# Up projections of the second layers' MLPs as seven products of quarter matrices, with weight sums made by DMA in DRAM

## The chip, the cores and the metric

One core of one Trainium2 chip runs the whole program. The metric is the device time of one execution in microseconds (us). The engines are PE (TensorE; PEld is its weight load), DVE (VectorE), ACT (ScalarE), POOL (GpSimd) and SP (SyncE, which only issues DMAs here). P is 128, S is 512 tokens, D is 1024.

## The reference

A block of a first type (pooling, stick-breaking attention, gates, an MLP) is followed by two layers of a second type. What the change touches is the MLP at the end of each second-type layer:

```python
D_FF_2 = 2816
    for l in range(DEPTH_2):                      # 2 layers
        ...
        h2 = _rmsnorm(x, g_ffn[l])
        z = _dwconv(h2 @ w_up[l], w_dw_ffn[l], b_dw_ffn[l])   # 1024 -> 5632, 3 taps along the tokens
        zg, zv = jnp.split(z, 2, axis=-1)
        x = x + (jax.nn.silu(zg) * zv) @ w_down[l]            # 2816 -> 1024
    return _rmsnorm(x, g_final)
```

All inputs and outputs are float32. The 5632 columns of `w_up` are 22 pairs of 128 gate columns and 128 value columns.

## The kernel before

Activations lie as [channels, tokens], so 1024 channels are eight tiles of 128x512. Every float32 product is made of three products of rounded parts: an operand is split into a high part `hi` (a cast to fp32r) and a low part `lo` (the remainder), and `mm3` (lines 376 to 380) issues hi·hi (L378), hi·lo (L379) and lo·hi (L380) into the same PSUM bank.

Weights come in units of eight blocks of 128x128, in the order in which PE uses them. `weight_plan` writes that order down as a list of units; the host packs the array `w` by it. `prep` brings one unit in: SP loads 512 KB into one of three `raw` buffers (L356), ACT casts it to `whi` (L357), POOL subtracts to get `wlo` (L358); `whi` and `wlo` have four buffers each. `take` hands out the next block and calls `prep` for units up to three ahead (`AHEAD`). There are 301 units. A unit's 24 products of 512 columns are PE's work between two units.

A scheduler orders each engine's queue: an instruction may be placed ahead of others that stand before it in the program, if it needs nothing from them. PE alone follows the program's order where `tc.manual_schedule` says so. Each queue then runs strictly in that order, and an instruction that waits for a semaphore holds what is behind it. DMAs that SP and ACT issue share eight completion semaphores in turn.

The program begins with `block1`: about 213 us of attention over eight heads, in which PE alternates between the heads (`scores`, `sums`, `weigh`, `mix_values`) and projections that fill its waits. ACT works there for each head through the three banks zC, zB, zA (L641, L342, L647), and this is what PE's next step waits for. Units 0 to 27 belong to this stretch. Its MLP and two calls of `layer2` follow.

At the end of `layer2` stands the MLP of the change. The first two column pairs are made by `proj_outer` (four banks at once, eight k steps), then `fin` gives the norm factor `r`; the other pairs are two `proj` of eight blocks each. Per pair, two multiplications by `r` (L1279), the three-tap filter `conv3` (L1282 to L1284) on both halves, a Silu, a product (L1298) and a split into `ah`, `al` (L446, L447) follow on ACT and DVE. After 11 pairs come the down projections into eight tiles of `x`, then the other 11 pairs.

## Time and profile before

| | |
|---|---|
| median of 3 runs | 1894.17 us (1893.68 to 1894.34) |
| profiled execution, its own time | 1894.09 us |
| its span, first to last instruction | 1892.4 us |
| mean granted TensorE clock | 0.994 |
| busy: PE, PEld, DVE, ACT, POOL | 97%, 79%, 51%, 50%, 50% |
| HBM read, written | 161.37 MB, 2.10 MB |

The page gives the busy time of each engine, then the span in 40 slices (a digit is the busy share in tenths), the DMA queues, the chain of work that ended last, and the costliest groups of instructions. Other views of the trace give one stretch: its instructions in order of time, its busy times, or who waited for whom. A matmul's printed duration overlaps the next one's, so PE's pace is read from the distance between starts.

### The profile page before, as it was taken

The page shows a single profiled execution, that of the slowest core. Times are in us where ns is not written, and L with a number is a line of the kernel's source. Part 1 is how long each engine was busy: PE and PEld are TensorE (multiplying, and loading weights), DVE is VectorE, ACT ScalarE, POOL GpSimd, SP SyncE. Part 2 cuts the span into 40 slices and gives each one's busy share as a digit, 9 for nine tenths or more (in the row PEclk, how much of TensorE's full clock was granted, in tenths as well). Part 3 has the DMA queues.
Part 4 walks back from the last instruction along what each step waited for, and adds up shares of the span by engine and source line. Part 5 has one row for each costly group of instructions (what it writes and reads, how often), then busy time and mean ns, then how long its engine had stood idle before and what let it go on. Part 6 is the DMA issues. An engine that isn't in the chain of part 4 may idle for free. (4 is left out here: it accounts for less than half of the span.)

```text
span 1892.4 us, 22115 instructions
## 1 busy us (share of the span) xinstructions
PE 1844.0 (97%) x8448; PEld 1500.1 (79%) x8448; DVE 959.7 (51%) x1420; ACT 948.1 (50%) x1442; POOL 937.1 (50%) x510
## 2 busy tenths in 40 slices
PE   8999999999999999899999999999999999999997
PEld 6877888888888888666788888888866788888886
DVE  4666552724032038996565225522998365405543
ACT  6766633633233347597554224434778554324442
POOL 5233444644444558665544444455866464444442
PEclk9999999999999999999999999999999999999999
DMA  5111224222222222200232222222210122222221
GB/s 186 68 56 61 79 101 140 89 101 91 99 100 90 100 79 90 78 27 23 87 110 93 97 101 97 92 100 93 97 39 23 61 101 100 92 98 100 95 96 56
DMA packets 48649, 164.89 MB, mean 87 GB/s; under 512 B 5536, under 2 KB 7584, under 8 KB 48544
## 3 DMA queue, kind: packets, MB, share of 16 engines
q1 hardware_dynamic: 46304, 160.34, 24.5%
q10 hardware_dynamic: 2240, 3.15, 0.5%
q8 instruction: 66, 1.08, 0.2%
q14 instruction: 39, 0.32, 0.1%
HBM read 161.37 MB, written 2.10 MB: 86 GB/s over the span
## 5 line engine op out<-in xcount | busy, mean ns | idle before, releaser
L358 POOL TENSOR_TENSOR wlo<-raw,whi 128x1024 fp32r<-128x1024 f32 x300 | 720.7, 2404 | 817.5 <-ACT whi L357 813.6
L357 ACT CAST whi<-raw 128x1024 fp32r<-128x1024 f32 (+1 forms) x302 | 313.7, 1040 | 507.5 <-PE b L379 412.7
L378 PE MATMUL b<-xh,whi 128*128 128x512 f32 (+1 forms) x1296 | 495.3, 382 | 2.7 <-ACT xh L449 2.7
L379 PE MATMUL b<-xl,whi 128*128 128x512 f32 (+1 forms) x1296 | 491.7, 379 | 3.4 <-DVE xl L450 3.3
L380 PE MATMUL b<-xh,wlo 128*128 128x512 f32 (+1 forms) x1296 | 491.3, 379 | 0.0
L379 PEld LDWEIGHTS b<-xl,whi 128*128 128x128 f32 x1296 | 244.3, 189 | 51.6 <-DVE xl L450 4.4
L378 PEld LDWEIGHTS b<-xh,whi 128*128 128x128 f32 x1296 | 244.2, 188 | 50.4 <-ACT xh L449 3.1
L380 PEld LDWEIGHTS b<-xh,wlo 128*128 128x128 f32 x1296 | 244.3, 189 | 45.9
L378 PE MATMUL b<-ah,whi 128*128 128x512 f32 (+1 forms) x646 | 243.6, 377 | 0.0
L379 PE MATMUL b<-al,whi 128*128 128x512 f32 (+1 forms) x646 | 243.2, 377 | 0.0
L380 PE MATMUL b<-ah,wlo 128*128 128x512 f32 (+1 forms) x646 | 243.2, 376 | 0.0
L380 PEld LDWEIGHTS b<-ah,wlo 128*128 128x128 f32 x646 | 121.6, 188 | 22.4
L378 PEld LDWEIGHTS b<-ah,whi 128*128 128x128 f32 x646 | 121.6, 188 | 22.3
L379 PEld LDWEIGHTS b<-al,whi 128*128 128x128 f32 x646 | 121.6, 188 | 22.2
L1218 POOL TENSOR_TENSOR cacc<-cacc,pd 128x510 f32<-128x510 f32 (+14 forms) x94 | 120.4, 1281 | 32.0 <-ACT pd L1216 28.3
L1206 DVE SCALAR_TENSOR_TENSOR cv<-u,vec,cv 128x497 f32<-128x497 f32 (+13 forms) x146 | 108.3, 742 | 7.7 <-ACT cv L1196 5.5
L1279 DVE TENSOR_TENSOR b<-b,r 128x512 f32<-128x512 f32 x88 | 61.0, 697 | 97.1 <-PE b L380 96.9
L1303 DVE TENSOR_TENSOR x<-x,b 128x512 f32<-128x512 f32 x30 | 20.6, 687 | 161.3 <-PE b L380 161.3
L446 ACT CAST ah<-cg 128x512 fp32r<-128x512 f32 x44 | 27.3, 621 | 98.7 <-DVE cg L1298 98.7
L378 PE MATMUL mm<-xh,whi 128*128 128x512 f32 x176 | 69.4, 394 | 0.0
L869 DVE TENSOR_TENSOR b<-rl,b 128x512 f32<-128x512 f32 x32 | 22.1, 695 | 92.6 <-ACT rl L868 92.6
L379 PE MATMUL mm<-xl,whi 128*128 128x512 f32 x176 | 68.8, 391 | 0.0
(430 smaller groups left out, 2851.1 us busy)
## 6 DMA issues: line engine op xcount, KB each, us to landing
raw<-w SPq DMA_DIRECT2D x295, 512.0 KB, 3.2
x<-xT SPq DMA_DIRECT2D x8, 256.0 KB, 6.6
x<-xT ACTq DMA_DIRECT2D x8, 256.0 KB, 4.8
raw<-w SPq DMA_DIRECT2D x7, 256.0 KB, 2.6
outT<-o ACTq DMA_DIRECT2D x4, 256.0 KB, 2.4
outT<-o SPq DMA_DIRECT2D x4, 256.0 KB, 2.5
vec<-vec SPq DMA_DIRECT2D x1, 363.0 KB, 6.9
f<-pos SPq DMA_DIRECT2D x1, 256.0 KB, 3.3
```

Source lines behind the costliest of these rows:

```text
L357: nc.scalar.copy(out=hi[:, cs], in_=raw[:, cs])
L358: (eng or nc.gpsimd).tensor_tensor(out=lo[:, cs], in0=raw[:, cs], in1=hi[:, cs].bitcast(F32), op=ALU.subtract)
L378: mm(ps, lhsT=wb[0], rhs=xb[0], start=start, stop=False, **kw)
L379: mm(ps, lhsT=wb[0], rhs=xb[1], start=False, stop=False, **kw)
L380: mm(ps, lhsT=wb[1], rhs=xb[0], start=False, stop=stop, **kw)
L446: nc.scalar.copy(out=hi, in_=src)
L869: V.tensor_tensor(out=ps, in0=rl, in1=ps, op=ALU.mult)
L1206: V.scalar_tensor_tensor(out=acc[:, o], in0=us[i][:, u], scalar=self.v("w_dw_conv_2", l, i * CONV_K + k), in1=acc[:, o], op0=ALU.mult, op1 ...
L1218: G.tensor_tensor(out=acc[:, o], in0=acc[:, o], in1=pd, op=ALU.add)
L1279: V.tensor_tensor(out=ps, in0=ps, in1=r, op=ALU.mult)
L1303: V.tensor_tensor(out=self.x[m], in0=self.x[m], in1=ps, op=ALU.add)
```

## The change

Nineteen of the 22 pairs of each layer (all but the first three, `PLAIN2`) are computed as a 2x2 block product in seven quarter products in place of eight. The weight of a pair is cut into four quarters of 512x128 (a11, a12 gate and value columns of the upper half of the 1024 channels; a21, a22 of the lower half), the normed activations into four quarters of 512x256 (halves of channels and of tokens). A quarter product is four blocks with 256 columns each, three matmuls per block.

- **Weights.** A new input `wq` holds the quarters. Four sums per pair are needed (S1 = a21 + a22, S3 = a11 + a21, S2 = S1 + a11, S4 = S2 + a12; the signs are put elsewhere). They are made in DRAM, for groups of four pairs (1.05 MB; the last group has three, 0.79 MB): a copy DRAM to DRAM issued from ACT, then a DMA issued from POOL that adds the second term to what the copy wrote. That is 20 copies and 20 adds for each layer, 40 and 40 in all. The program calls them one by one from `prep`, from unit 24 on, every second unit for layer 0 and every third for layer 1.
- **Units.** A pair takes 28 blocks in place of 16, so there are 359 units in place of 301. A unit with quarters is loaded by two or three DMAs of 2 KB rows.
- **Activations.** `quarter_inputs` makes the seven right-hand operands (four normed quarters and their differences, each split into parts), on DVE, ACT and POOL, while PE runs `proj_outer` for the three plain pairs (six banks). The matmul that sums the squares now stands after two of the eight k steps.
- **Pairs.** A pair's products accumulate in two banks, and intermediate sums are read out while the bank goes on being filled: three half-bank copies on ACT (`snap`), three half-bank adds on DVE. The multiplications by `r` are gone for these pairs. PE runs the last two products of a pair between those of the next one.
- **Chunks** are 8, 7 and 7 pairs in place of 11 and 11, so three rounds of down projections; the first three tiles of a round are interleaved. The order on PE is now written by hand for the whole MLP.

```diff
-CHUNK2 = 11
+CHUNKS2 = (0, 8, 15, 22)
+PLAIN2 = 3
+NDOWN = 3
+SUM_PAIRS = 4
+SUMS = ("S1", "S2", "S3", "S4")
+QUARTERS = ("a11", "a12", "a21", "a22")
+SIDE_FROM, SIDE_STEPS = 24, (2, 3)
...
+        ffn = [("w_up_2", l, P * k, _span(P * f + o)) for k in range(KT) for f in range(PLAIN2) for o in (0, FF2)]
+        for ks in chunks2():
+            quarter = lambda which, f: [(which, l, f, kk) for kk in range(KT // 2)]
+            before = None
+            for f in ks:
+                if f >= PLAIN2:
+                    ffn += quarter("a11", f) + quarter("a12", f)
+                    if before is not None:
+                        ffn += quarter("a22", before)
+                    ffn += quarter("S2", f) + quarter("S1", f)
+                    if before is not None:
+                        ffn += quarter("S4", before)
+                    ffn += quarter("S3", f)
+                    before = f
+            down = [("w_down_2", l, P * k, _span(P * m)) for k in ks for m in range(NDOWN)]
+            ffn += down[:4] + quarter("a22", before) + down[4:8] + quarter("S4", before) + down[8:]
+            ffn += [("w_down_2", l, P * k, _span(P * m)) for m in range(NDOWN, KT) for k in ks]
+        add(ffn)
...
+def pack_quarters(inputs):
+    w = inputs["w_up_2"].reshape(NL, 2, KT // 2, P, 2, NF2, P)[:, :, :, :, :, PLAIN2:]
+    w = w.transpose(0, 4, 1, 5, 3, 2, 6)
+    return np.ascontiguousarray(w).reshape(NL, 4, NF2 - PLAIN2, P, KT // 2 * P)
...
+        if eng is None and any(b[0] in QUARTERS + SUMS for b in self.plan[u]):
+            for c0, c1, src in self.sources(u):
+                nc.sync.dma_start(out=raw[:, c0:c1], in_=src)
...
+        if u >= SIDE_FROM and self.side and u % SIDE_STEPS[self.side[0][0]] == 0:
+            self.side.popleft()[1]()
...
+    def sources(self, u):
+        out = []
+        for b, (name, l, f, kk) in enumerate(self.plan[u]):
+            if name in QUARTERS:
+                src = self.wq[l, QUARTERS.index(name), f - PLAIN2]
+            elif name in SUMS:
+                reg, i = divmod(f - PLAIN2, SUM_PAIRS)
+                src = self.sum_of[l, name, reg].rearrange("r (x c) -> (r x) c", c=KT // 2 * P)[i * P : (i + 1) * P]
...
+        nc = self.nc
+        pool = ctx.enter_context(self.tc.tile_pool(name="sums", bufs=1, space=bass.MemoryType.DRAM))
+        self.sum_of = {}
+        row = 2048
+        n = NF2 - PLAIN2
+        for l in range(NL):
+            regs = [(i, min(i + SUM_PAIRS, n)) for i in range(0, n, SUM_PAIRS)]
+            quarter = lambda name, r: self.wq[l, QUARTERS.index(name), r[0] : r[1]].rearrange("a p c -> (a p c)").rearrange("(r c) -> r c", c=row)
+            def copy(dst, src):
+                return lambda: nc.scalar.dma_start(out=dst, in_=src)
+            def add(dst, src):
+                return lambda: nc.gpsimd.dma_start(out=dst, in_=src, accum_op=ALU.add, max_dma_last_dim=row)
+            for g, r in enumerate(regs):
+                for name in SUMS:
+                    self.sum_of[l, name, g] = pool.tile([(r[1] - r[0]) * P * KT // 2 * P // row, row], F32, name=f"{name}_{l}_{g}")
+            for first, more in ((("S1", "a21"), "a22"), (("S3", "a11"), "a21"), (("S2", "S1"), "a11"), (("S4", "S2"), "a12")):
+                name, base = first
+                for g, r in enumerate(regs):
+                    self.side.append((l, copy(self.sum_of[l, name, g], self.sum_of[l, base, g] if base in SUMS else quarter(base, r))))
+                for g, r in enumerate(regs):
+                    self.side.append((l, add(self.sum_of[l, name, g], quarter(more, r))))
...
+        op_ = tc.tile_pool(name="quarters", bufs=1, side="right", reuse_waits="tile")
+        ops = self.quarter_tiles(op_.__enter__())
+        hp_ = tc.tile_pool(name="hp", bufs=1, reuse_waits="tile")
+        hp = hp_.__enter__()
+        rs = []
+        def norms():
+            rs.append(fin(pp, "b", True))
+            self.quarter_inputs(hp, ops, "g_ffn_2", l, rs[0][1])
+        pss = self.proj_outer(pp, "b", acts, 2 * PLAIN2, between=norms)
+        r = rs[0][0]
...
+        def unit(f, pg, pv, wv):
+            cg = conv3(pg, self.v("w_dw_ffn_2", l, 3 * f, 3), f, "cg")
+            cv = conv3(pv, wv, NF2 + f, "cv")
+            self.act(AF.Silu, out=pg, in_=cg)
+            V.tensor_tensor(out=pg, in0=pg, in1=cv, op=ALU.mult)
+            return self.split(fp, pg, ("ah", "al"))
...
+                def snap(ps):
+                    t = fp.tile([P, S // 2], F32, name="snap", bufs=4)
+                    A.copy(out=t, in_=ps)
+                    return t
+                def times(ps, name, start, stop):
+                    hi, lo = ops[name]
+                    for kk in range(KT // 2):
+                        self.mm3(ps, self.take(), (hi[:, kk], lo[:, kk]), start and kk == 0, stop and kk == KT // 2 - 1, skip_group_check=True)
+                def p4(g):
+                    times(g["v"][:, L], "T4", False, True)
+                    V.tensor_tensor(out=g["v"][:, R], in0=g["g"][:, R], in1=g["u3"], op=ALU.add)
+                def p3(g):
+                    times(g["g"][:, R], "B22", False, True)
+                    V.tensor_tensor(out=g["g"][:, R], in0=g["g"][:, R], in1=g["u2"], op=ALU.add)
+                    a.append(unit(g["f"], g["g"], g["v"], self.wneg[l][:, 3 * g["f"] : 3 * g["f"] + 3]))
+                old = None
+                for f in ks:
+                    if f < PLAIN2:
+                        continue
+                    g = {"f": f, "v": pp.tile([P, S], F32, name="b"), "g": pp.tile([P, S], F32, name="b")}
+                    times(g["v"][:, L], "B11", True, False)
+                    u1 = snap(g["v"][:, L])
+                    times(g["g"][:, L], "B21", True, True)
+                    V.tensor_tensor(out=g["g"][:, L], in0=g["g"][:, L], in1=u1, op=ALU.add)
+                    if old is not None:
+                        p4(old)
+                    times(g["v"][:, L], "T2", False, False)
+                    g["u2"] = snap(g["v"][:, L])
+                    times(g["g"][:, R], "T1", False, False)
+                    if old is not None:
+                        p3(old)
+                    times(g["v"][:, L], "T3", False, False)
+                    g["u3"] = snap(g["v"][:, L])
+                    old = g
+                ds = [pp.tile([P, S], F32, name="b") for _ in range(NDOWN)]
+                def down(n0, n1):
+                    for n in range(n0, n1):
+                        k, m = divmod(n, NDOWN)
+                        self.mm3(ds[m], self.take(), a[k], k == 0, k == len(ks) - 1)
+                down(0, 4)
+                p4(old)
+                down(4, 8)
+                p3(old)
+                down(8, NDOWN * len(ks))
...
+        for k in range(0, KT // 2, 2):
+            h = []
+            for k0 in (k, KT // 2 + k):
+                t = pool.tile([P, 2, S], F32, name=f"h{len(h)}")
+                for j in range(2):
+                    V.scalar_tensor_tensor(out=t[:, j], in0=self.x[k0 + j], scalar=self.v(gname, l, k0 + j), in1=r, op0=ALU.mult, op1=ALU.mult)
+                h.append(t)
+            (b11, b12), (b21, b22) = ((t[:, :, L], t[:, :, R]) for t in h)
+            def put(name, src, eng):
+                hi, lo = (t[:, k : k + 2] for t in ops[name])
+                A.copy(out=hi, in_=src)
+                eng.tensor_tensor(out=lo, in0=src, in1=hi.bitcast(F32), op=ALU.subtract)
+            def temp():
+                return pool.tile([P, 2, S // 2], F32, name="t", bufs=3)
+            put("B11", b11, G)
+            put("B21", b21, G)
+            t1 = temp()
+            V.tensor_tensor(out=t1, in0=b11, in1=b12, op=ALU.subtract)
+            t2 = temp()
+            V.scalar_tensor_tensor(out=t2, in0=t1, scalar=-1.0, in1=b22, op0=ALU.mult, op1=ALU.subtract)
+            put("T2", t2, V)
+            put("T1", t1, V)
+            t3 = temp()
+            V.tensor_tensor(out=t3, in0=b22, in1=b12, op=ALU.subtract)
+            put("T3", t3, V)
+            V.scalar_tensor_tensor(out=t2, in0=t2, scalar=-1.0, in1=b21, op0=ALU.mult, op1=ALU.subtract)
+            put("T4", t2, V)
+            put("B22", b22, G)
```

The order of instructions on two engines shows where the scheduler puts the new DMAs. POOL, from the start of the weight units (`wlo` is one unit's low part, `pt` a step of the pooling). Before:

```order
L577 MEMSET sq 128x384
L283 MEMSET e_117 1x1
L583 MEMSET sq 128x128
L578 MEMSET sq 128x128
L579 AFFINE_SELECT sq<-sq 128x128
L584 AFFINE_SELECT sq<-sq 128x128
L358 TENSOR_TENSOR wlo<-raw,whi 128x1024 x13
L696 COPY pt<-z 128x1
L358 TENSOR_TENSOR wlo<-raw,whi 128x1024 x5
```

After, in the same queue, where 30 of the 40 adds (`S_` is a sum in DRAM, with layer and group) and 14 units stand before these rows, and two adds right behind them:

```order
L402 TENSOR_TENSOR wlo<-raw,whi 128x1024
L446 DMA S_1_0_159<-wq 512x512
L402 TENSOR_TENSOR wlo<-raw,whi 128x1024
L446 DMA S_1_1_163<-wq 512x512
L446 DMA S_1_2_167<-wq 512x512
L446 DMA S_1_3_171<-wq 512x512
L446 DMA S_1_4_175<-wq 384x512
L446 DMA S_1_0_161<-wq 512x512
L402 TENSOR_TENSOR wlo<-raw,whi 128x1024
L446 DMA S_1_1_165<-wq 512x512
L446 DMA S_1_2_169<-wq 512x512
L402 TENSOR_TENSOR wlo<-raw,whi 128x1024
```

The adds have moved far ahead of the units from which the program calls them: all 40 stand before the `wlo` of unit 19, the first before that of unit 1.

ACT, at the attention's fourth head (`x<-zC`, `x<-zB` are steps of its bank work, `whi` a unit's high part). Before:

```order
L641 ACTIVATE x<-zC 128x512
L684 COPY ot<-av 64x512
L342 ACTIVATE x<-x 128x512 x2
L647 CAST x<-x 128x512
L641 ACTIVATE x<-zB 128x384
L342 ACTIVATE x<-x 128x384 x2
L357 CAST whi<-raw 128x1024
L647 CAST x<-x 128x384
L641 ACTIVATE x<-zA 128x512
```

After:

```order
L746 ACTIVATE x<-zC 128x512
L443 DMA S_1_1_165<-S_1_1_163 16x16384
L380 ACTIVATE x<-x 128x512
L789 COPY ot<-av 64x512
L380 ACTIVATE x<-x 128x512
L443 DMA S_1_2_169<-S_1_2_167 16x16384
L752 CAST x<-x 128x512
L443 DMA S_1_3_173<-S_1_3_171 16x16384
L746 ACTIVATE x<-zB 128x384
L401 CAST whi<-raw 128x1024
L380 ACTIVATE x<-x 128x384
L443 DMA S_1_4_177<-S_1_4_175 16x12288
```

The last of the 40 copies, S4 from S2 of layer 1, stands inside the zB step of the fourth head; S2 of that group must have had its add by then. No copy and no add stands later in either queue.

ACT again, in the MLP's pairs of layer 0. Before:

```order
L357 CAST whi<-raw 128x1024
L1282 ACTIVATE cg<-b,vec 128x512
L342 ACTIVATE cg<-cg 128x512
L357 CAST whi<-raw 128x1024
L1282 ACTIVATE cv<-b,vec 128x512
L446 CAST ah<-cg 128x512
```

After:

```order
L401 CAST whi<-raw 128x1024 x2
L1399 ACTIVATE cg<-b,vec 128x512
L1427 COPY snap<-b 128x256
L401 CAST whi<-raw 128x1024
L380 ACTIVATE b<-cg 128x512
L1427 COPY snap<-b 128x256
L545 CAST ah<-b 128x512
L401 CAST whi<-raw 128x1024
L1399 ACTIVATE cv<-b,vec,wneg_124 128x512
L1427 COPY snap<-b 128x256
```

Between the casts of a pair's units, three `snap` copies have come in, for which PE waits before it goes on filling the same half bank.

## Rows read from the trace of the kernel before

**Rows 1.** The page, busy time of each engine: microseconds (share of the span) x instructions.
```profile
PE 1844.0 (97%) x8448; PEld 1500.1 (79%) x8448; DVE 959.7 (51%) x1420; ACT 948.1 (50%) x1442; POOL 937.1 (50%) x510
```
**Rows 2.** The page, 40 slices of 47 us: busy tenths, and bandwidth.
```profile
PE   8999999999999999899999999999999999999997
...
DMA  5111224222222222200232222222210122222221
GB/s 186 68 56 61 79 101 140 89 101 91 99 100 90 100 79 90 78 27 23 87 110 93 97 101 97 92 100 93 97 39 23 61 101 100 92 98 100 95 96 56
```
**Rows 3.** Layer 0's MLP: busy of each engine, clock, DMA share, GB/s.
```profile
957.90:1084.00 126.10, 126.10 (x558) 104.46 (x557) 66.12 (x92) 52.63 (x67) 55.27 (x23) 1.00 0.28 96
1084.00:1146.00 62.00, 62.00 (x276) 51.34 (x275) 17.33 (x24) 19.67 (x23) 26.75 (x12) 1.00 0.29 101
```
**Rows 4.** Waits in the whole span: line, releaser, us in total, times, longest.
```profile
SPq L356 <- POOL wlo L358: 1702.9, 297, 30.5
...
POOL wlo L358 <- ACT whi L357: 813.6, 255, 9.5
...
ACT whi L357 <- PE b L379: 412.7, 176, 4.4
```
**Rows 5.** PE in order of time, 512 columns: start, printed duration; nine starts apart.
```profile
1854.75 0.39 PE L380 MATMUL b<-ah,wlo 128*128 128x512 f32 x1
...
1856.79 0.39 PE L380 MATMUL b<-ah,wlo 128*128 128x512 f32 x1
```
**Rows 6.** PE in order of time, 256 columns: thirty-two starts apart.
```profile
1866.05 0.28 PE L379 MATMUL b<-al,whi 128*128 128x256 f32 x1
...
1869.88 0.28 PE L378 MATMUL b<-ah,whi 128*128 128x256 f32 x1
```
**Rows 7.** Groups between 950 and 1160 us: busy, mean ns of one | idle before.
```profile
L358 POOL TENSOR_TENSOR wlo<-raw,whi 128x1024 fp32r<-128x1024 f32 x39 | 93.5, 2398 | 118.0 <-ACT whi L357 118.0
...
L357 ACT CAST whi<-raw 128x1024 fp32r<-128x1024 f32 x38 | 40.0, 1052 | 74.7 <-PE b L379 73.7 <-PE b L380 1.0
...
L1282 ACT ACTIVATE cv<-b,vec 128x512 f32<-128x512 f32 x15 | 11.5, 770 | 0.3 <-DVE b L1279 0.3
...
L1283 DVE SCALAR_TENSOR_TENSOR cv<-b,vec,cv 128x511 f32<-128x511 f32 x15 | 11.2, 747 | 10.8 <-ACT cv L1282 10.8
...
L342 ACT ACTIVATE cg<-cg 128x512 f32<-128x512 f32 x15 | 9.5, 632 | 18.8 <-DVE cg L1284 18.8
L446 ACT CAST ah<-cg 128x512 fp32r<-128x512 f32 x15 | 9.3, 621 | 32.6 <-DVE cg L1298 32.6
```
**Rows 8.** DVE before layer 0's MLP in order of time: start, time of the run.
```profile
927.03 9.70 DVE L450 SCALAR_TENSOR_TENSOR xl<-x,vec,xh 128x512 fp32r<-128x512 f32 x5
936.65 0.68 DVE L1261 TENSOR_TENSOR x<-x,mm 128x512 f32<-128x512 f32 x1
...
939.62 0.68 DVE L461 TENSOR_TENSOR acc<-acc,sq 128x512 f32<-128x512 f32 x1
```
**Rows 9.** Two stretches at the start of the program, columns as in Rows 3.
```profile
8.00:12.00 4.00, 4.00 (x13) 3.12 (x12) 2.08 (x3) 3.60 (x7) 0.92 (x1) 1.00 1.03 401
0.00:125.00 125.00, 113.92 (x531) 93.32 (x532) 71.97 (x94) 83.03 (x135) 46.92 (x38) 1.00 0.33 113
```
**Rows 10.** ACT at the fourth head in order of time.
```profile
116.35 0.49 ACT L641 ACTIVATE x<-zB 128x384 f32<-128x384 f32 x1
116.87 1.08 ACT L342 ACTIVATE x<-x 128x384 f32<-128x384 f32 x2
118.51 1.06 ACT L357 CAST whi<-raw 128x1024 fp32r<-128x1024 f32 x1 [0.56 <-PE mm L379]
```
**Rows 11.** POOL in order of time, units 18 and 19.
```profile
119.64 2.37 POOL L358 TENSOR_TENSOR wlo<-raw,whi 128x1024 fp32r<-128x1024 f32 x1 [6.70 <-ACT whi L357]
129.74 0.45 POOL L696 COPY pt<-z 128x1 f32<-128x1 f32 x1 [7.72 <-DVE plzA L672]
130.91 0.69 POOL L696 COPY pt<-pt 128x2 f32<-128x2 f32 x1 [0.71 <-ACT whi L357]
131.56 2.86 POOL L358 TENSOR_TENSOR wlo<-raw,whi 128x1024 fp32r<-128x1024 f32 x1
```
**Rows 12.** Line L380, `mm` tile of the attention's fillings: duration min/median/max ns, first and last start.
```profile
L380 PE MATMUL mm<-xh,wlo x176: 388/389/397, 32.3 to 210.1; 128*128 128x512 f32 x176
```

More of the change, by code (lines that the diff above doesn't have):

```diff
@@ L76, in _span, with chunks2 @@
     return np.arange(c0, c0 + n)
+def chunks2():
+    return [range(a, b) for a, b in zip(CHUNKS2, CHUNKS2[1:])]
 def weight_plan():
@@ new lines, in sums @@
+    def sums(self, ctx):
+        nc = self.nc
[3 more added lines that the diff above has]
+        n = NF2 - PLAIN2
+        for l in range(NL):
+            regs = [(i, min(i + SUM_PAIRS, n)) for i in range(0, n, SUM_PAIRS)]
[13 more added lines that the diff above has]
+                    self.side.append((l, add(self.sum_of[l, name, g], quarter(more, r))))
@@ L405, in proj_outer @@
             for k, a in enumerate(acts):
+                if k == OUTER_LAG + 1 and between is not None:
+                    between()
                 for ps in pss:
@@ L504, in split, with finish @@
                 self.sq_add(acc[:, cs], x, i == 0, nc.gpsimd if i < on_pool else nc.vector)
-        def finish(pp, tag):
+        def finish(pp, tag, both=False):
             r = self.rp.tile([P, S], F32, name="r", bufs=1)
-            self.rsqrt(r, self.total(pp, tag, acc)[0], D)
-            return r
+            tot = self.total(pp, tag, acc)[0]
+            if not both:
+                self.rsqrt(r, tot, D)
+                return r
+            self.rsqrt(r, tot, D, tot)
+            nc.scalar.copy(out=r, in_=tot)
+            return r, tot
         return acts, split, finish
@@ new lines, in layer2 @@
+        L, R = HALVES
+        last_chunk = len(chunks2()) - 1
+        with tc.manual_schedule(engines={mybir.EngineType.PE}):
+            for c, ks in enumerate(chunks2()):
+                a = []
+                for f in ks:
+                    if f >= PLAIN2:
+                        break
+                    pg, pv = pss[2 * f : 2 * f + 2]
+                    for ps in (pg, pv):
+                        V.tensor_tensor(out=ps, in0=ps, in1=r, op=ALU.mult)
+                    a.append(unit(f, pg, pv, self.v("w_dw_ffn_2", l, 3 * (NF2 + f), 3)))
+                def snap(ps):
[14 more added lines that the diff above has]
+                old = None
+                for f in ks:
+                    if f < PLAIN2:
+                        continue
+                    g = {"f": f, "v": pp.tile([P, S], F32, name="b"), "g": pp.tile([P, S], F32, name="b")}
[23 more added lines that the diff above has]
+                down(8, NDOWN * len(ks))
+                tail = 2 if l == NL - 1 and c == last_chunk else 0
+                for m in range(KT - tail):
+                    ps = ds[m] if m < NDOWN else self.proj(pp, "b", a)
+                    V.tensor_tensor(out=self.x[m], in0=self.x[m], in1=ps, op=ALU.add)
+                if tail:
+                    self.final(pp, a)
@@ L1365, in arrays @@
         "w": pack_weights(inputs, weight_plan()),
+        "wq": pack_quarters(inputs),
         "vec": pack_vectors(inputs),
```

82 lines of the change are left out of this document (43 added, 39 removed).

## The prediction

> **What bounds the kernel now.** I read the page first. PE is busy for 1844.0 of 1892.4 us, no other engine for more than 51% [rows 1], and the slices show PE full everywhere while DMA is a fifth to a third used after the first slice [rows 2]. In layer 0's MLP PE is busy for all of 126.10 and 62.00 us, at granted clock 1.00, the higher of its two levels (2.4 GHz), with POOL at 44% and DMA at 0.28 [rows 3]. The waits say the same from the other side: SP waits for POOL to free a raw buffer, POOL for ACT's cast, ACT for PE to give back a weight buffer [rows 4]. So PE's stream of matmuls is the time, weights wait for it, and a change pays by what it takes off PE, as long as weights keep coming.
>
> **The gain on PE.** Nine starts of 512-column matmuls span 2.04 us, 0.227 us each [rows 5]. Thirty-two starts of 256-column ones span 3.83 us, 0.120 us each, more than half [rows 6]. A pair costs 48 x 0.227 = 10.9 us now and 7 x 4 x 3 = 84 x 0.120 = 10.1 us after. That is 0.8 us for each of 38 pairs, **-30.4 us**; the columns alone (one eighth fewer) would have promised 1.36 us for each.
>
> The Trainium skill (TensorE: Matmul & The Clock Gate, section Back-to-back issue gap) gives the start-to-start distance as N/2.4 + 2.5 ns, so 216 and 109 ns. By that a pair would go from 10.4 to 9.2 us and the sum would say -45 us; the rows show 227 and 120 [rows 5, 6], so I stay with them.
>
> **Weights in the pairs.** A unit of quarters lasts 24 x 0.120 = 2.9 us on PE, in place of 5.4. POOL needs 2.40 us for it, ACT 1.05 us for the cast [rows 7]. Per pair POOL then works 3.5 x 2.40 = 8.4 of 10.1 us; ACT 3.5 x 1.05 + 2 x 0.77 + 0.63 + 0.62, and three half-bank copies at half of a 0.62 us cast, 7.4 us. Both fit. DMA goes to 524 KB per 2.9 us, 182 GB/s, against 401 that it has shown [rows 9]. I cost the stream at nothing; its cover is 1.7 us of POOL per pair.
>
> **Entry into the pairs.** `quarter_inputs` puts 24 operations on DVE ahead of the plain pairs' work, and ACT's first `snap`, which PE's third quarter product waits for, stands behind four filter steps that need that DVE work. The sum of squares is ready at 939.62 + 0.68 = 940.3, PE's outer stretch begins at about 936.7 [rows 8], so the moved matmul (36 x 0.227 = 8.2 us in, at 945) waits for nothing, and r is there five short steps on ACT and DVE later (about 0.7 us each, as those of [rows 7]), at about 950. DVE then needs 24 x 0.75 = 18 us [rows 7] or, at the pace of 9.70 us for five next to a busy POOL [rows 8], 47 us; some 5 us of filter steps follow. PE reaches the wait at 936.7 + 144 x 0.227 + 2.9 = 972. That is a wait of 1 to 30 us; I take 10 (DVE at 1.1 us, as POOL is half busy there), for two layers **+20 us** (2 to 60). The rest of the MLP's order I cost at zero: the last pair of a chunk has 10 to 13 interleaved down steps of 0.68 us before its result is needed, about what its chain takes.
>
> **The sums in DRAM.** This is the big term. The copies and adds read only weights, so the scheduler has moved all 80 to the front: the order shows all 40 adds in POOL's queue ahead of unit 19's `wlo`, and all 40 copies in ACT's ahead of the end of the fourth head's zB step. In the trace of before ACT reaches that place at 117 us [rows 10], POOL its place between 122 and 130 us [rows 11]. The program's own pacing (every second or third unit) plays no part. The last copy reads S2 of layer 1 after its add, so by then at least 35 copies and 35 adds have landed. These queues are not free to run ahead of that: ACT's next step of the attention stands behind the copy, and PE behind ACT.
>
> Bytes: 19 pairs x 128 x 512 x 4 = 4.98 MB per sum and layer, 39.9 MB for all copies, 34.9 MB for 35 of 40. No row shows a transfer DRAM to DRAM or an accumulating one. The nearest are loads DRAM to SBUF: 401 GB/s where the engines are full, and over the first 125 us 113 GB/s at share 0.33, which is 342 GB/s for a full engine set and 41 us of full work [rows 9]. I take a copy as one pass through the DMA engines like a load, and an add as two, since both terms are read. Then 35 copies are 34.9/0.401 = 87 us, 35 adds 174 us, own loads up to 117 us some 34 us: 295 us of DMA work has to be done at a place that was reached at 117 us, **+178 us**; at 342 GB/s it is 102 + 204 + 40 = 346, **+229 us**. I take the middle, **+205 us**. POOL's and ACT's time for issuing, and the small transfers' latency, hide under the transfers.
>
> Bounds. From below: an add costs no more than a copy, 87 + 87 + 34 - 117 = +91 us. Less needs transfers faster than any row. From above: a byte costs by its crossings of the memory, twice for a copy, three times for an add: 174 + 261 + 34 - 117 = +352 us.
>
> The Trainium skill (Collectives: The Full Stack, section The bandwidth ceiling) says that a reducing DMA step runs at half of a copying one, because it reads two sources; an estimate by it is the two passes that I take. No run here shows it yet.
>
> **Sum.** 1894.1 (the profiled execution; its span is 1.7 us shorter, the median 0.1 longer) - 30.4 + 20 + 205 = 2088.7, say **2089 us**, slower.
>
> **Rivals.**
>
> *Faster: the transfers stay hidden.* If 295 us of DMA work took less than the 117 us that the queues leave, only -30.4 + 20 (or + 2) would remain: about 1884 us, 1866 at best. For it speaks the DMA share of 0.33 in these 125 us [rows 9], with two thirds idle; but idle time there is 84 us, and 35 copies alone fill it. It decides where the mean of the 70 transfers falls under (117 - 34)/70 = 1.2 us, 840 GB/s, twice the peak of the rows. Chance 0.06, most of it for a misread order.
>
> *An add is a copy.* The addition rides along in one pass: 1894 - 30 + 20 + 91 = 1975 us. For it: DMA engines in the rows are paced by what they move, and an add writes no more than a copy. Against it: it reads twice. Chance 0.14, of which 0.02 is for prices so low that nothing measurable is left.
>
> *Memory crossings decide.* Copies at half the load rate, adds at a third: 1894 - 30 + 20 + 352 = 2236 us. For it: all rows are of loads, which touch DRAM once. Against it: nothing in the rows is near a memory limit. Chance 0.24. The Trainium skill (DMA: Bandwidth & Descriptors, section Latency and other measured facts) gives 207 to 214 GB/s per direction for copies DRAM to DRAM, the half rate that this rival needs; no row here shows such a copy.
>
> *The pairs starve.* POOL at 83% cannot hold its pace, and each quarter unit takes 3.3 us in place of 2.9: 133 units, +53 us on the sum, 2142 us. It lies inside the range. Chance 0.1, taken out of the main case.
>
> **How the numbers follow.** Main case, 2000 to 2200 us: 0.46, with the starved pairs 0.56. Cheap adds 0.14, crossings 0.24, faster 0.06. The range has to reach both neighbours: below, -30.4 + 2 + 91 gives 1957; above, -30.4 + 60 + 352 gives 2276, which I round up to 2300 as the price of an add is unknown. Within 0.2% (3.8 us, about what a measurement of this kernel can tell from no change) is that tail of the cheap adds: 0.02. Faster 0.06, slower 0.92.
>
> **What would show it.** In the profile after, the attention's last filling matmul, at 210.1 us before [rows 12], should stand near 415; DMA digits at 9 from the first slice until then, back to 2 afterwards; PE digits down to 4 to 6 there, with the granted clock at its lower level in places where PE stands. In the waits POOL and ACT DMA issues should wait for DMAs. From there to the first MLP of the second type nothing moves. In the pairs, 84 matmuls should take 10.1 us, with one wait per layer at the first pair. The forecast is wrong if that matmul stays near 210 us, or if POOL's queue shows the adds at another place; it is right for the wrong reason if the time is lost in the pairs.

## The result and the profile after

The changed kernel takes 2117.2 us (2114.3 to 2120.0) beside 1894.1 for the kernel before: ratio 1.118, 95% interval 1.116 to 1.120. It is slower by 223 us; 2089 had been predicted, with a range of 1957 to 2300. The first profiled execution was a disturbed one (mean granted clock 0.81, 2247 us), so the lines below are from a second profiled execution of the same kernel, e1_again: 2127.5 us, span 2125.8.

The page, busy times, then rows of the 40 slices (53 us each); they answer to [rows 1, 2]:

```profile
PE 1845.9 (87%) x9792; PEld 1548.5 (73%) x9792; DVE 1008.3 (47%) x1522; ACT 1054.2 (50%) x1644; POOL 1135.8 (53%) x622
...
PE   8321517999999999999999799999999997999997
...
PEclk9666758999999999999999899999999998999999
DMA  9999998123232323222002254545321022436351
```

PE is busy for as long as before, 1846 against 1844 us; what has grown is the time in which it stands, nearly all of it in slices 2 to 7, where DMA is full. The same in windows (PE, PEld, DVE, ACT, POOL busy, granted clock, DMA share, GB/s), as [rows 9]:

```profile
0.00:56.00 56.00, 46.25 (x198) 37.52 (x199) 27.63 (x34) 29.29 (x44) 28.55 (x34) 1.00 0.96 310
56.00:112.00 56.00, 14.91 (x48) 10.93 (x46) 7.49 (x9) 9.99 (x17) 9.73 (x7) 0.65 1.06 274
...
168.00:224.00 56.00, 7.94 (x30) 6.12 (x28) 2.33 (x4) 3.05 (x5) 9.98 (x10) 0.56 1.06 254
...
280.00:336.00 56.00, 13.72 (x42) 10.17 (x43) 5.86 (x9) 9.30 (x16) 13.35 (x10) 0.62 1.08 242
336.00:392.00 56.00, 54.66 (x267) 45.76 (x268) 34.39 (x48) 36.89 (x64) 20.07 (x13) 0.98 0.56 137
```

From 56 to 336 us PE is busy for 86 of 280 us (the sum of five windows, of which three stand here), beside DMA engines that are full; behind that it is the other way round. The attention's last filling matmul, at 210.1 us in [rows 12], stands here (duration min/median/max, first and last start):

```profile
L477 PE MATMUL mm<-xh,wlo x176: 388/394/628, 35.3 to 426.2; 128*128 128x512 f32 x176
```

This execution is 233 us longer than the profiled one of before. 216 of them are lost by 426 us, and the other 17 behind the attention: from its last filling matmul to the end 1700 us pass in place of 1682. The copies' own line shows the same 216 us: the last of the 40 is issued at 333.0 us, at a place in ACT's queue that was reached at 117 us before [rows 10]:

```profile
L443 ACTq DMA_DIRECT2D S<-S x20: 475/476/1996, 61.7 to 333.0; - x20
```

Who waited, from the waits of the whole span (us in total, times, longest):

```profile
POOL S L446 <- issue: 202.7, 23, 33.4
...
PE zA L762 <- ACT x L752: 103.0, 2, 52.0
...
ACT x L380 <- DMA S<-wq: 60.1, 5, 35.6
...
ACT qh L716 <- DMA S<-wq: 44.5, 1, 44.5
```

ACT's steps of the attention stand behind copies that wait for an add, and PE behind ACT. POOL's weight work stands behind adds; for the 203 us before these the profile names no releaser (its "issue").

### The profile page after: what moved, and what is told of

Same layout as the page of the kernel before. It is cut to its first block, busy times and chain, and to the rows that moved or that the text cites. A ratio compares the mean times of both kernels' runs of the same rounds, so it can differ in the third digit from the quotient of the medians.

```text
span 2244.9 us, 25952 instructions
## 1 busy us (share of the span) xinstructions
PE 1996.2 (89%) x9792; PEld 1611.8 (72%) x9792; DVE 1009.8 (45%) x1522; ACT 1058.3 (47%) x1644; POOL 1135.7 (51%) x622
## 3 DMA queue, kind: packets, MB, share of 16 engines
q0 software_dynamic: 20096, 39.85, 10.2%
## 4 chain that ended last, share of the span: by engine, by line
PE 76%; issue 8%; DVE 8%; DMA 4%; POOL 2%; ACT 1%; SPq 0%; DVEq 0%; ACTq 0%; POOLq 0%
PE b L475 20%; PE b L476 20%; PE b L477 20%; DMA S<-wq 3%; PE s L1241 3%; PE mm L475 2%; PE mm L476 2%; PE mm L477 2%; PE t L1258 1%; DVE xl L549 1%; POOL wlo L402 1%; POOL S L446 1%; PE av L1264 1%; PE cv L577 1%; PE av L1263 1%
## 5 line engine op out<-in xcount | busy, mean ns | idle before, releaser
L402 POOL TENSOR_TENSOR wlo<-raw,whi 128x1024 fp32r<-128x1024 f32 (+1 forms) x358 | 863.3, 2414 | 731.8 <-ACT whi L401 722.5
L401 ACT CAST whi<-raw 128x1024 fp32r<-128x1024 f32 (+1 forms) x360 | 373.6, 1038 | 595.2 <-PE b L476 449.0
L475 PE MATMUL b<-xh,whi 128*128 128x512 f32 (+1 forms) x688 | 276.3, 402 | 6.4 <-DVE x L1366 3.9
L476 PE MATMUL b<-xl,whi 128*128 128x512 f32 (+1 forms) x688 | 271.8, 395 | 2.3 <-DVE xl L549 2.3
L477 PE MATMUL b<-xh,wlo 128*128 128x512 f32 (+1 forms) x688 | 271.7, 395 | 0.0
L475 PE MATMUL b<-ah,whi 128*128 128x512 f32 (+1 forms) x638 | 258.9, 406 | 0.0
L475 PEld LDWEIGHTS b<-xh,whi 128*128 128x128 f32 x688 | 133.7, 194 | 42.7 <-DVE x L1366 4.9
L476 PEld LDWEIGHTS b<-xl,whi 128*128 128x128 f32 x688 | 133.8, 195 | 38.5 <-DVE xl L549 2.9
L446 POOL DMA_DIRECT2D S<-wq x40 | 41.5, 1096 | 235.1 <-issue 188.4
L477 PEld LDWEIGHTS b<-xh,wlo 128*128 128x128 f32 x688 | 133.8, 194 | 32.7
```

Source lines behind the costliest of these rows:

```text
L401: nc.scalar.copy(out=hi[:, cs], in_=raw[:, cs])
L402: (eng or nc.gpsimd).tensor_tensor(out=lo[:, cs], in0=raw[:, cs], in1=hi[:, cs].bitcast(F32), op=ALU.subtract)
L446: return lambda: nc.gpsimd.dma_start(out=dst, in_=src, accum_op=ALU.add, max_dma_last_dim=row)
L475: mm(ps, lhsT=wb[0], rhs=xb[0], start=start, stop=False, **kw)
L476: mm(ps, lhsT=wb[0], rhs=xb[1], start=False, stop=False, **kw)
L477: mm(ps, lhsT=wb[1], rhs=xb[0], start=False, stop=stop, **kw)
```

## The experiments

"Excess" below is worked out from PE's starts: the sum of their distances over the 170 us that begin with the first matmul of the projection ahead of the MLP (`mm<-uh`), less 0.227 us for each 512-column and 0.120 us for each 256-column matmul. The stretch takes in the entry into the pairs. In the kernel before the excess is 0.3 us in either layer. e1_again, e4_sums_only, e5_no_add and e12_copies are one execution each.

### The transfers: what they cost

**e1_again** is the changed kernel once more, without an edit.

> The changed kernel itself, once more, for a trace at the clock that its three fast executions had (mean 0.936 to 0.939). All theories: 2114 to 2120 us. By the queue-order theory (the copies and adds stand in the attention and fill the DMA engines there) the attention's last filling matmul starts at 400 to 425 us, DMA is full until 320 to 340 us, and behind the attention the program is some 10 us shorter than before (gain of 30 us in the pairs, less about 10 us of waits at the entry of each of the two layers). By the rival (the pairs lose too) the part behind the attention is longer than before's 1682 us.

It gave the trace above, 2127.5 us. DMA is full until 336 us, as the theory of the filled front wants, and 426.2 us is just above its range. But the part behind the attention became longer, 1700 us against 1682, and that is what the rival had said: the pairs lose too.

**e4_sums_only** is the kernel before with the transfers alone; **e12_copies** drops the adds from it, **e5_no_add** turns them into copies on POOL's queue:

```diff
+        if u >= SIDE_FROM and self.side and u % SIDE_STEPS[self.side[0][0]] == 0:
+            self.side.popleft()[1]()
...
+        k.sums(ctx)
```

```diff
-                for g, r in enumerate(regs):
-                    self.side.append((l, add(self.sum_of[l, name, g], quarter(more, r))))
```

```diff
-                return lambda: nc.gpsimd.dma_start(out=dst, in_=src, accum_op=ALU.add, max_dma_last_dim=row)
+                return lambda: nc.gpsimd.dma_start(out=dst, in_=src, max_dma_last_dim=row)
```

> The kernel before with the 80 transfers added in the same way, and their sums read by nobody; they stand at the same places of POOL's and ACT's queues as in the change. Queue-order theory: 2117 - 1884 + 1894 = 2127 us (2100 to 2150), all of it ahead of 430 us. Rival (the loss is shared by attention and pairs): 2000 to 2080 us.

> e4_sums_only without its 40 adds: the kernel before with the 40 copies alone in front of ACT's queue. From e5_no_add (80 copies) and e4_sums_only (40 copies and 40 adds) a copy takes 3.0 us and an add 4.8 us if 83 us of transfers are free: 40 copies are 120 us, 37 over, 1930 us. If a copy runs at the pace of a load (1 MB in 2.5 us, the prediction), 40 are 100 us, and the time is 1911 us; if nothing but the queue's order counts, 1893 us.

> The kernel before with the same 80 transfers at the front of the queues as in e4_sums_only, but each of the 40 adds is a plain copy of the same quarter into the same place, on the same queue of POOL (the sums aren't used, so the outputs are those of before). In e4_sums_only the transfers and the loads beside them held the attention up by 227 us beyond the 83 us that they had free, 310 us of transfers. Two passes for an add (the prediction): 40 copies and 40 adds are three units of 103 us, 80 copies two, so 103 us go and the time is about 2018 us. An add costs what a copy costs: nothing goes, 2121 us. Crossings of memory decide (two for a copy, three for an add): 310 us are five units of 62 us, 80 copies are four, so 62 us go, 2059 us.

e4_sums_only took 2121.3 us, as expected: with no pair changed, the transfers alone cost 227 us, and its attention's last filling matmul stands at 436.5 us, 226 later than before. e12_copies took 1942.6, 49 over before, where 37 were expected, and e5_no_add 2050.1, between the 2018 of two passes and the 2059 of crossings, and nearer to the latter. So 40 adds are worth 2121.3 - 1942.6 = 178.7 us, 4.5 us each, and 40 further copies 107.5 us, 2.7 us each: a ratio of 1.66. The DMA queues' own time says it too. First e1_again from 0 to 336 us, then e5_no_add from 0 to 300 us (packets, MB, share of 16 engines; q0 is POOL's queue, q10 ACT's):

```profile
q0 software_dynamic: 18410, 36.53, 63.8%
q10 hardware_dynamic: 1242, 39.06, 30.3%
```

```profile
q0 software_dynamic: 10368, 39.85, 44.2%
```

In e1_again, 36.53 MB of adds occupy 0.638 x 336 = 214 us of the full set of engines, 170 GB/s, and 39.06 MB of copies 102 us, 384 GB/s. In e5_no_add copies on POOL's queue take 133 us for 39.85 MB, 300 GB/s. An add is thus 1.76 times a copy of its own queue and 2.25 times one of ACT's. Copies at 300 and 384 GB/s are far above half the load rate of 401, so the rival "memory crossings" falls by its price of a copy. The ratio that it gives, 3 to 2, is not excluded in the same way: 1.66 and 1.76 lie between its 1.5 and the 2 of two passes. The packets differ as well, 2.0 KB each for adds and 3.8 KB for POOL's copies, by the rows above. Small packets alone do not make an add slow: in the pair of e3_nosums below, loads of quarters (1133 packets, 2.06 MB) move 210 GB/s at a DMA share of 0.64, which is 328 GB/s for a full set.

By its section The bandwidth ceiling, the Trainium skill (Collectives: The Full Stack) lets a reducing DMA step run at half of a copying one; these runs give 1.66 to 2.25, around it. The Trainium skill (DMA: Bandwidth & Descriptors, Latency and other measured facts) gives 207 to 214 GB/s per direction for copies DRAM to DRAM of tiles whose rows lie apart; here contiguous ones ran at 384 GB/s of engine time.

### The transfers: where they run

**e2_placed** keeps each transfer behind the weight work of the unit that calls it, a copy behind ACT's cast, an add behind POOL's subtraction; **e11_away** changes, in e2_placed, the units alone:

```diff
-            self.side.popleft()[1]()
+            self.side.popleft()[1](cast, rest)
-                return lambda: nc.scalar.dma_start(out=dst, in_=src)
+                return lambda cast, rest: self.issue_behind(nc.scalar.dma_start(out=dst, in_=src), cast)
```

```diff
-SIDE_FROM, SIDE_STEPS = 24, (2, 3)
+SIDE_UNITS = set(range(24, 144, 2)) | set(range(230, 270, 2))
```

> One edit: each copy stays behind the cast, and each add behind the POOL subtraction, of the unit whose loading calls it, so that the 80 transfers are spread over units 24 to 222 as the program text paces them. Queue-order theory: one transfer per 11 to 16 us, up to unit 146, hides beside the weights, and the time is 1885 us (1866 to 1900); in layer 0's pairs, where 26 of them fall, they may cost up to 10 us. Rival (the bytes cost wherever they run, since sums and weights share 16 engines): 80 times 1.5 to 3 us stay, 2000 to 2120 us.

> e2_placed with another pacing alone: layer 0's 40 copies and adds at every second unit from 24, 20 of layer 1's behind them up to unit 142, the other 20 between the two layers' pairs (units 230 to 268), so that none runs while pairs run. Theory: the 32 us that e2_placed lost against e3_nosums are late weights in layer 0's pairs, and go: 1911 to 1915 us. Rival: they are the transfers' price wherever they run: 1935 to 1943 us.

e2_placed took 1943.1 us, ratio 1.026 (1.024 to 1.027): 174 us came back, and the attention ended at 210.9 us, but 58 us were missing to the 1885 expected. e11_away took 1917.5, ratio 1.013 (1.011 to 1.014), where 1911 to 1915 were expected: 6 over e3_nosums below, which has no transfers. A stretch of layer 0's MLP (pairs and a round of down projections) in the one and in the other, columns as above:

```profile
1060.00:1180.00 120.00, 112.97 (x759) 104.34 (x758) 41.79 (x69) 54.70 (x79) 81.08 (x37) 0.97 0.76 222
```

```profile
1060.00:1180.00 120.00, 120.00 (x822) 110.65 (x821) 47.11 (x76) 59.42 (x83) 81.57 (x35) 1.00 0.46 150
```

Transfers beside the pairs bring the DMA share to 0.76, and PE loses 7 of 120 us; without them PE is full. POOL has the same work in both, so it isn't POOL that starves PE. It is late weights: between 1010 and 1300 us of e2_placed ACT's casts wait 46 us for loads in 20 waits, the first of three rows of them being

```profile
ACT whi L401 <- DMA raw<-wq: 23.4, 8, 4.5
```

and in e11_away these waits come to 2 us, in three. PE waits in its turn for the `snap` that stands behind the cast in ACT's queue. The rule "every third unit" put 25 of layer 1's 40 transfers beside layer 0's MLP (980 to 1370 us), where a unit of quarters lasts half as long.

### The pairs alone

**e3_nosums** leaves the transfers out; its products read plain quarters, so the computation is not the reference's:

```diff
-                reg, i = divmod(f - PLAIN2, SUM_PAIRS)
-                src = self.sum_of[l, name, reg].rearrange("r (x c) -> (r x) c", c=KT // 2 * P)[i * P : (i + 1) * P]
+                src = self.wq[l, SUMS.index(name), f - PLAIN2]
-        k.sums(ctx)
```

> The copies and adds are left out; a plain quarter of the weights is read in the place of each sum, so the values of the pairs are wrong and all else of the change stands. It gives the price of the pairs alone. Queue-order theory: 1894 - 30 + 20 = 1884 us (1866 to 1900). Rival (the pairs starve, POOL at 83%): 1915 us or more, with PE waiting for POOL throughout the pairs.

It took 1911.3 us, ratio 1.010 (1.008 to 1.011): the pairs by themselves lose 17 us where a gain of 10 was expected. In layer 0's pairs PE is as quick as promised; two starts of the same step of neighbouring pairs, 84 matmuls apart:

```profile
1129.98 0.28 PE L472 MATMUL b<-B21h,whi 128*128 128x256 f32 x1
...
1139.88 0.28 PE L472 MATMUL b<-B21h,whi 128*128 128x256 f32 x1
```

9.90 us, against 10.9 for a pair before. POOL works in these 9.90 us for 8.51, and PE is full (columns as above):

```profile
1129.98:1139.88 9.90, 9.90 (x87) 9.90 (x85) 6.13 (x11) 7.57 (x11) 8.51 (x5) 1.00 0.64 210
```

The loss is at the entry. PE's waits from 930 to 1010 us:

```profile
PE b L472 <- ACT snap L1424: 8.3, 1, 8.3
PE b L472 <- DVE b L1449: 7.2, 1, 7.2
PE b L472 <- DVE x L1363: 2.8, 1, 2.8
```

and ACT in order of time, up to the snap that PE had waited for since 981.7:

```profile
984.96 0.62 ACT L1505 CAST T4h<-t 128x512 fp32r<-128x512 f32 x1 [4.10 <-DVE t L1522]
985.48 1.04 ACT L401 CAST whi<-raw 128x1024 fp32r<-128x1024 f32 x1
986.94 0.78 ACT L1396 ACTIVATE cg<-b,vec 128x512 f32<-128x512 f32 x1 [0.42 <-DVE b L1419]
987.62 0.77 ACT L1396 ACTIVATE cv<-b,vec 128x512 f32<-128x512 f32 x1
988.28 0.77 ACT L1396 ACTIVATE cg<-b,vec 128x512 f32<-128x512 f32 x1
988.94 0.78 ACT L1396 ACTIVATE cv<-b,vec 128x512 f32<-128x512 f32 x1
989.60 0.38 ACT L1424 COPY snap<-b 128x256 f32<-128x256 f32 x1
```

The snap stands behind four filter steps, and these behind the last quarter input on DVE. The second wait is DVE's addition of that snap, which stands behind the filters of the plain pairs until 999.7 us. After the long wait PE runs at the lower of its two levels (1.2 GHz) for a while, as the windows behind it show:

```profile
981.00:990.00 9.00, 0.74 (x7) 0.54 (x5) 8.32 (x11) 4.62 (x8) 5.12 (x2) 0.73 0.20 59
990.00:994.00 4.00, 2.93 (x12) 2.63 (x12) 4.00 (x7) 2.57 (x4) 2.37 (x1) 0.50 0.42 131
```

The excess is 24.7 us in layer 0 and 20.8 in layer 1.

**e7_order** changes the order there in e3_nosums (the same part of the computation is left out): the plain pairs come inside the first pair, their filter's ACT steps behind its snap, the third quarter input behind the first plain pair's scaling on DVE, the last two behind its product, and the bank that the last residual addition still reads is kept for the sum of squares (an excerpt):

```diff
+            if behind is not None:
+                self.issue_behind(first, behind)
...
+                    if f == PLAIN2:
+                        snapped = self.snapped
+                        last = plain(0, snapped)
...
+                    if f == PLAIN2:
+                        rs[1](last, snapped)
...
+                        rs[2](self.product)
...
+                            plain(n)
```

> e3_nosums (no copies or adds, a plain quarter read in place of each sum, so values are wrong) with another order at the entry into the pairs: the first snap stands ahead of the plain pairs' filter steps on ACT, the third, fourth and last quarter inputs come behind the first plain pair's product on DVE, and the bank that the last residual add still reads is kept for the sum of squares. Theory: the 25 us that PE waits per layer at the first pair are queue order; they fall under 8 us per layer, 1877 us or a little less. Rival: DVE simply has too much work between the norm and the second pair, and the wait moves from the first pair to the second: 1900 to 1911 us.

1895.2 us, ratio 1.001 (1.000 to 1.002): 16 us came back, not 34. The excess fell to 14.4 and 13.4 us, not under 8; the long waits are gone, and shorter ones (3.7 and 1.8 us) stand at T1 and B21 of the second pair. The order of the queues was some two fifths of the loss. The rest has moved to the second pair, as the rival had it.

### The address of the tiles

A stretch whose code the change doesn't touch, from the first down projection of the first-type MLP to the last matmul ahead of the second-type layer's `cqh` products, takes 355.3 us in e3_nosums (434.6 to 789.9) and 351.2 before (430.2 to 781.4). **e6_shift** adds to the kernel before the change's two constant tiles, and nothing else:

```diff
+        for l in range(NL):
+            t = c.tile([P, 3 * NF2], F32, name=f"wneg{l}")
+            nc.gpsimd.tensor_scalar(out=t, in0=self.v("w_dw_ffn_2", l, 3 * NF2, 3 * NF2), scalar1=-1.0, scalar2=None, op0=ALU.mult)
```

> The kernel before, with nothing but the two small constant tiles that the change adds (66 words a partition each, here written once and never read). They move the weight tiles by 576 bytes against the activations at the other end of SBUF. Theory: a 512-column matmul whose moving operand and weights lie differently modulo 512 bytes starts every 233.3 ns in place of 227.0, as in the changed kernels; that falls on the projections of the norms' outputs in the attention stages and in the first-type MLP, some 1700 matmuls where PE is the bound, so +9 to +14 us, about 1905 us. Rival: the slower matmuls of the changed kernels come from something else (their other transfers, the quarter tiles, the clock), and two unused tiles do nothing: 1894 us.

1905.2 us, ratio 1.006 (1.0045 to 1.0075), as expected: two unused tiles cost 11.8 us. PE in order of time in e6_shift, first where it reads `xh`, which has stayed in place while the weights moved (nine starts apart), then where it reads `ah`, which moved with them (nine starts apart):

```profile
560.02 0.40 PE L381 MATMUL b<-xh,whi 128*128 128x512 f32 x1
...
562.12 0.39 PE L381 MATMUL b<-xh,whi 128*128 128x512 f32 x1
```

```profile
449.96 0.39 PE L381 MATMUL b<-ah,whi 128*128 128x512 f32 x1
...
452.00 0.39 PE L381 MATMUL b<-ah,whi 128*128 128x512 f32 x1
```

2.10 us and 2.04 us: 0.233 and 0.227 us each, the latter as in [rows 5]. In the built programs `xh` lies at 480 modulo 512 bytes; the weights at 480 before, and at 32 here.

### Towards a version that is faster

**e8_all** puts together the units of e11_away, the order of e7_order (the last quarter inputs behind another step, the second and third plain pair further back on DVE, the outer stretch's last two columns behind the first four for two steps), constants padded to a whole multiple of 512 bytes, and 64 bytes (`pad`) that move the quarter tiles; **e9_aligned** leaves the `pad` out of it (an excerpt):

```diff
-            t = c.tile([P, 3 * NF2], F32, name=f"wneg{l}")
+            t = c.tile([P, P], F32, name=f"wneg{l}")[:, : 3 * NF2]
...
+        pool.tile([P, 16], F32, name="pad")
...
+                        rs[2](first_lo)
```

> The changed kernel with four repairs together: its copies and adds pinned behind their units, layer 0's 40 at every second unit from 24 and layer 1's half before layer 0's pairs and half behind them, none while pairs run; the order of e7_order at the entry, with the second and third plain pair further back on DVE and the outer stretch's last two columns behind the first four for its first two steps; the constant tiles padded to 1024 bytes, so that whole matmuls read aligned again, and the quarter tiles moved by 64 bytes. Theory: the losses are separate and add up. From 1895 us of e7_order, the address gives back some 11 us (e6_shift), the rest of the entry's 13 us per layer some 9, and the transfers cost 0 to 5 us away from the pairs: 1866 to 1871 us, faster than before by 1.2 to 1.4%. Rival: the transfers cost time wherever they run (e2_placed lost 32 us to them, 12 to 20 of it while layer 0's pairs ran); then 1885 to 1900 us.

> e8_all without the 64 bytes: the quarter tiles then lie like the weights modulo 512 bytes. In the traces 256-column matmuls start every 120 ns where both lie alike and every 117.5 ns where they lie 64 bytes apart, the reverse of 512-column ones. Theory: the offset alone does it, and 3192 matmuls at 2.5 ns make e9_aligned 8 us slower than e8_all. Rival: the 117.5 ns come from the pairs' order or operands, and the two kernels take the same time within 2 us.

e8_all took 1891.9 us, ratio 0.999 (0.998 to 1.000), where 1866 to 1871 were expected, and e9_aligned 1903.9, 1.006 (1.004 to 1.007). Not the transfers kept the gain away, as the rival had it: the projection ahead of layer 0's second-type MLP starts at 908.9 us (906.7 before), and from 1060 to 1180 us, among the pairs, PE is busy for 120.00 of 120.00 us. The excess at the entry is 15.1 and 20.0 us. PE's waits from 930 to 1010 us in e8_all:

```profile
PE b L481 <- DVE T3l L1526: 3.1, 2, 1.8
PE b L480 <- DVE b L1445: 2.9, 1, 2.9
PE b L481 <- DVE T4l L1526: 1.8, 1, 1.8
PE b L480 <- DVE x L1372: 0.9, 1, 0.9
```

All are DVE's, at other places than in e7_order: what is brought forward on DVE pushes something else back. Losses that share an engine don't add up. e9_aligned's 12 us fit the offset, where 8 were expected of it. Its 256-column starts in the pairs are 120.0 ns apart on average (distances over 0.2 us left out), e8_all's 116.3, and over 3192 matmuls that makes 12 us. Only 8.2 of them show at the end of the two traces (the last matmul ends at 1889.8 against 1881.6 us); the medians of all executions differ by 11.9. In e8_all whole runs of pairs keep one of two paces. Beside the 9.90 us seen above there is this one, again 84 matmuls apart:

```profile
1084.32 0.28 PE L480 MATMUL b<-B21h,whi 128*128 128x256 f32 x1
...
1093.84 0.28 PE L480 MATMUL b<-B21h,whi 128*128 128x256 f32 x1
```

That is 9.52 us, 0.113 us a matmul. By the starts, 88 of e8_all's 266 quarter products have this pace, 30 in e3_nosums, 113 in e1_again, none in e9_aligned. What decides between the two, no run shows.

**e10_six** gives DVE more cover: six plain pairs a layer, three of them behind the outer stretch, so that 16 of 22 pairs are left as seven products. It also makes the quarter inputs without a pause and keeps only the last two plain pairs inside the first two pairs (an excerpt):

```diff
-PLAIN2 = 3
+PLAIN2 = 6
+NOUTER = 3
+                        if f + NOUTER < PLAIN2:
+                            pss += [self.proj(pp, "b", acts) for _ in range(2)]
-SIDE_UNITS = set(range(24, 144, 2)) | set(range(230, 270, 2))
+SIDE_UNITS = set(range(24, 120, 2)) | set(range(228, 260, 2))
```

> e8_all with six plain pairs a layer in place of three (three in the outer stretch, three behind it), 16 of 22 pairs as seven products, and the quarter inputs made without a pause. Theory: what is left of the entry's loss (15 and 20 us per layer in e8_all) is DVE's work between the norm and the second pair, some 27 us of quarter inputs and 20 us of filters, which three plain pairs on PE do not cover; three pairs more are 33 us of cover, the excess falls under 5 us per layer, and the three pairs lose 3 us of gain: 1892 - 30 + 6 = 1868 us, faster than before by 1.3%. Rival: DVE stays behind anyway, since in the pairs its filters and additions take 8 of 10 us, and the waits only move on: 1885 to 1895 us.

1868.2 us, ratio 0.987 (0.985 to 0.988): 25 us faster than before, and what had been expected. The excess is 0.7 and 1.9 us, almost that of before. Cover and order were changed together here, and no run has one without the other. PE's only wait from 930 to 1050 us, and the windows of layer 0's pairs:

```profile
PE b L483 <- DVE x L1375: 0.4, 1, 0.4
```

```profile
990.00:1060.00 70.00, 69.89 (x391) 61.05 (x390) 29.44 (x46) 30.44 (x41) 42.85 (x18) 1.00 0.42 136
1060.00:1180.00 120.00, 120.00 (x854) 112.78 (x853) 45.44 (x74) 61.77 (x89) 83.53 (x36) 1.00 0.48 153
```

## Why the prediction was right, and where it was not

**The sums in DRAM: right.** The step predicted +205 us, between 178 and 229. The changed kernel less e3_nosums is 2117.2 - 1911.3 = 206 us, and e4_sums_only 227 on its own. The place was right: the time is lost where the transfers fill DMA, with ACT and POOL behind them and the clock down where PE stands. The prices were right in the main. A copy ran at 384 GB/s, and an add, taken as two passes at 401 or 342 (200 or 171 GB/s), at 170. With these rates the step's own sum is 91 us for 35 copies, 205 for 35 adds and 34 for loads, less 117: +213. The free time was taken too high: 40 copies alone cost 49 us, where 104 us of them less 83 free ones would cost 21. In e12_copies the engines are only 82 to 92% full until 168 us, and no run follows this up. So it is partly luck that the middle of two prices came within 1 us of 206, a difference of two kernels of which one varies between 2114 and 2127 us from execution to execution. Of the rivals, "an add is a copy" (1975) and "memory crossings" (2236) both fell, the latter by its price of a copy.

**The gain on PE: too small.** -30.4 us from 0.120 us a matmul; most pairs of e3_nosums run at 0.118, 9.90 us, so 38 x 1.0 = -38. The rows of 256 columns [rows 6] were of tiles that lie like the weights, and those of the quarters don't. The pairs at 9.52 us make it 1 to 2 us more in e3_nosums and some 6 in e1_again.

**Entry into the pairs: too small, and the mis-sized term.** +20 us were taken from a range of 2 to 60; the excess of 24.7 and 20.8 us less the 0.3 of before is 45. The step counted DVE's 24 operations and one wait behind them, and these it had right: the 24 take 27.4 us in e3_nosums (958.8 to 986.2), 1.14 us each where 1.1 was assumed, and the wait for the first `snap` is 8.3 us in layer 0 and 6.9 in layer 1, where 10 was taken. It put three things at nothing: the second wait, of 7.2 us in each layer, in which product T1 waits for an addition that stands behind three plain pairs' filters on DVE; the one at the outer stretch's fifth bank (2.8 and 2.9 us); and the lower clock after the waits (0.63 from 948 to 952 us, 0.50 from 990 to 1003). So 22 us per layer came in place of 10.

**"From there to the first MLP of the second type nothing moves": wrong.** A price of zero had been put on the constants, and their 576 bytes cost 6 to 8 us up to there (the projection ahead of layer 0's second-type MLP starts at 915.1 us in e3_nosums and at 913.0 in e7_order; 906.7 before), 11.8 in all in e6_shift.

**The starved pairs: no.** POOL does have the reckoned load there, 8.51 of 9.90 us (86%; 83% was forecast), but it holds its pace: without transfers beside the pairs PE is full.

**The sum.** -38 + 45 + 206 make 213 of the 223 us, and the 10 that remain fit the address (8 to 12). The prediction put 195 there; it was near since the one large term was right, and its three small ones were off by 8, 25 and 8 to 12 us.

## What to carry to other kernels

A transfer that reads only weights has no place of its own: unless it is tied to one, a scheduler moves all of them to the front, and everything queued behind them on their engines pays (206 us here, 6 once each was tied to a unit away from the hungry stretches). A shorter product on PE pays only where the vector work that makes its inputs is covered; count all the work that an engine has between the last thing it waits for and the second round, and give it cover. New orders alone (e7_order, e8_all) moved the waits; more cover, together with a simpler order, ended them (e10_six). And after adding a small constant, compare a stretch that wasn't touched: its pace tells whether tiles have moved against each other.

## What the runs showed of the hardware

- Matmuls care about how their operands lie against each other. With 512 columns, starts are 0.227 us apart where moving tile and weights are alike modulo 512 bytes, and 0.233 where they are 64 bytes off; with 256 columns it is the other way, 0.120 alike, and 0.118 or 0.113 off (e6_shift, e8_all, e9_aligned). Other offsets weren't tried. The Trainium skill (TensorE: Matmul & The Clock Gate, Back-to-back issue gap) gives by N/2.4 + 2.5 one distance for each size, 216 and 109 ns; no row here reaches either.
- An accumulating transfer DRAM to DRAM ran at 170 GB/s of engine time (e1_again), a plain one at 300 on POOL's queue (e5_no_add) and at 384 on ACT's (e1_again).
- PE that stood for 8.3 us went on at the lower level: granted clock 0.50 over the next 4 us in e3_nosums, and 256-column starts 0.213 us apart there in place of 0.118, so that a wait costs more than its length.
